# Rotating images by 180 degrees: one group loaded in four interleaved parts, and a store that waits for the third of them

## The chip, the cores and the metric

The kernel runs on one core of a Trainium2 chip. The metric is device time in microseconds (us) of one execution. The profile is one execution of the same program, taken by the hardware profiler; its span is the time from the first to the last instruction, and what lies around the span is in the metric too.

## The reference

```python
def setup_inputs():
    batch, c, h, w = 32, 3, 256, 256
    return {"x": np.random.randn(batch, c, h, w).astype(np.float32)}

def reference(x):
    return np.rot90(x, k=2, axes=(-2, -1)).astype(np.float32)
```

A rotation by 180 degrees turns both axes of each 256x256 image round. Seen as one line of 65,536 numbers, each of the 96 images is reversed. There is no arithmetic: 25.2 MB are read, reversed and written.

## The kernel before

Each image is cut into four rows of E = 16384 numbers (64 KB), which gives 384 rows. They form three groups of 128 rows, and each group fills one tile of 128 partitions by 16384 columns: A, Bt and Ct (lines 38 to 40). The first two groups take the even and the odd rows of the first 256 (`x4[0]`, `x4[1]`), the third takes the last 128 rows in order (`x4[2]`, line 34). A fourth tile T (128 x 2048, J = 2048) is for exchanging.

Loads: A and then Ct are issued from the SP queue (SyncE), Bt from the ACT queue, each as one transfer over all 128 partitions (lines 64 to 67). A memset of a few columns of Bt (line 65) stands ahead of Bt's load, which waits for it. All three loads are in the queues within the first 2 us.

Reversal: each row of a tile is reversed in place by VectorE. `swap(t, lo, w)` (line 56) exchanges w columns from the left with the w columns at the mirrored place on the right, in three copies: right part reversed into T, left part reversed to the right, T to the left. `turn(t, lo, hi)` (line 69) does this in widths of at most 2048 from the outside inward; `turn(t, 0, half)`, with half = 8192, reverses the whole row. So the last columns that are exchanged are the innermost ones, next to column 8192. All copies are on line 47 and are kept in the order of the program.

Stores: what is left is to turn the order of the four rows of an image, and the output's access pattern does that (line 54, `[:, ::-1, lo:hi]`). All stores are issued from the SP queue, behind the loads of A and Ct. SP is in order: a store that waits holds back the stores behind it.

The order of lines 76 to 84, which is also VectorE's order: three quarters of A (widths 1 to 3); the store of A's first LEAD = 256 columns, which needs only the first width; MID = 2432 columns of Bt; the last width of A; the store of the rest of A (16128 columns); the rest of Bt and its store; Ct and its store.

Of the kernel before, what the change touches and what calls it, by code (L numbers as in the profile page):

```python
# [2 lines left out]

os.environ.setdefault("NEURON_RT_ULTRASERVER_MODE", "4")

# [4 lines left out]


@with_exitstack
def kernel(
    ctx: ExitStack,
    tc: tile.TileContext,
    x: bass.AP,
    out: bass.AP,
):
    nc = tc.nc  # L20
    P = 128

    B, C, H, W = x.shape
    L = H * W
    G = 32
    E = L // 4
    J = E // 8

    xr = x.rearrange("b c h w -> (b c) (h w)").rearrange(
        "m (s e) -> (m s) e", s=4)  # L30
    om = out.rearrange("b c h w -> (b c) (h w)").rearrange(
        "m (s e) -> m s e", s=4)
    rows = 2 * P
    x4 = [xr[0:rows:2], xr[1:rows:2], xr[rows:rows + P]]
    o4 = [om[0:2 * G, 1::2], om[0:2 * G, 0::2], om[2 * G:3 * G]]

    pool = ctx.enter_context(tc.tile_pool(name="slots", bufs=1))
    A = pool.tile([P, E], x.dtype, tag="A")
    Bt = pool.tile([P, E], x.dtype, tag="B")
    Ct = pool.tile([P, E], x.dtype, tag="C")  # L40
    T = pool.tile([P, J], x.dtype, tag="T")

    def back(t, lo, hi):
        return t[:, hi - 1:(lo - 1 if lo else None):-1]

    def copy(dst, src):
        tc.keep_in_program_order(nc.vector.tensor_copy(out=dst, in_=src))  # L47

    def load(t, g, lo, hi, queue=nc.sync):
        return queue.dma_start(out=t[:, lo:hi], in_=x4[g][:, lo:hi])  # L50

    def store(t, g, lo, hi):
        return nc.sync.dma_start(
            out=o4[g][:, ::-1, lo:hi], in_=t[:, lo:hi])

    def swap(t, lo, w):
        hi = E - lo - w
        copy(T[:, 0:w], back(t, hi, hi + w))
        copy(t[:, hi:hi + w], back(t, lo, lo + w))
        copy(t[:, lo:lo + w], T[:, 0:w])  # L60

    MID = 2432
    LEAD = 256
    load(A, 0, 0, E)
    nc.vector.memset(Bt[:, 0:256], 0.0)  # L65
    load(Bt, 1, 0, E, nc.scalar)
    load(Ct, 2, 0, E)

    def turn(t, lo, hi):
        while lo < hi:  # L70
            w = min(J, hi - lo)
            swap(t, lo, w)
            lo += w

    half = E // 2
    turn(A, 0, half - J)
    store(A, 0, 0, LEAD)
    turn(Bt, 0, MID)
    turn(A, half - J, half)
    store(A, 0, LEAD, E)  # L80
    turn(Bt, MID, half)
    store(Bt, 1, 0, E)
    turn(Ct, 0, half)
    store(Ct, 2, 0, E)


# [1 line left out]
_INS = ['x']  # L88
_OUTS = [((32, 3, 256, 256), 'float32')]


# [23 lines left out]
```

## Time and profile before

| | us |
|---|---|
| median of 3 runs (121.79 to 121.88) | 121.8 |
| the profiled execution | 121.81 |
| its span | 120.0 |
| VectorE busy | 44.9 |
| VectorE's wait for the load of A | 38.4 |
| issue of the store of A's first 256 columns | 43.30 |
| issue of the store of the rest of A | 59.62 |
| issue of the store of Bt | 70.37 |
| issue of the store of Ct | 85.50 |

The profile was taken on the one core that runs; PEclk and the like play no part, since TensorE has no work. In the views, "SPq" is SyncE's queue, where DMAs are issued; q1 is the DMA queue fed by SP, q10 the one fed by ACT. In a view by windows, the columns are the window, its length, the busy time of VectorE and GpSimd with the number of instructions in it, the granted clock, the DMA share and the rate. A packet of 64 KB, which is one row, is booked in full in the window in which it starts, so the share of a short window can be above 1 or be 0. The time "to landing" of a DMA runs from the start of its issue to the last of its completion signals.

### The profile page before, as it was taken

To read this page: it belongs to the slowest core of one execution; us is meant where nothing else is said; L and a number is where in the kernel's file an instruction comes from. 1 tells how busy PE (TensorE), PEld (TensorE's weight loads), DVE (VectorE), ACT (ScalarE), POOL (GpSimd) and SP (SyncE) were. 2 spreads that over 40 slices of the span, in tenths; PEclk is the share of its full clock that TensorE was granted. 3 is DMA by queue.
4 is the path that set the end of the run, shared out by engine and by line. 5 is a ranking of instruction groups with operands and counts; after the bars stand their busy time and mean duration, and the time that the engine had idled before them with its cause. 6 is when DMAs were issued, how large, how long until landed. Compare 5 with 4: busy or idle time off the path is not lost.

```text
span 120.0 us, 97 instructions
## 1 busy us (share of the span) xinstructions
DVE 44.9 (37%) x40; POOL 0.2 (0%) x4
## 2 busy tenths in 40 slices
DVE  0000000000000899999999999999400000000000
POOL 0000000000000000000000000000000000000000
DMA  9888988898889888998899777988898889888990
GB/s 349 349 349 349 699 349 349 349 677 371 349 349 677 371 349 349 568 481 349 349 388 688 344 344 344 688 349 349 349 699 349 349 349 699 349 349 349 655 393 0
DMA packets 1008, 50.33 MB, mean 419 GB/s; under 512 B 112, under 2 KB 240, under 8 KB 240
## 3 DMA queue, kind: packets, MB, share of 16 engines
q1 hardware_dynamic: 864, 41.94, 81.4%
q10 hardware_dynamic: 144, 8.39, 16.1%
HBM read 25.17 MB, written 25.17 MB: 419 GB/s over the span
## 4 chain that ended last, share of the span: by engine, by line
DVE 38%; DMA 32%; issue 1%
DMA A<-in_x_dram 32%; DVE T L47 13%; DVE Bt L47 9%; DVE A L47 8%; DVE Ct L47 8%
## 5 line engine op out<-in xcount | busy, mean ns | idle before, releaser
L47 DVE COPY T<-A 128x2048 f32<-128x2048 f32 x4 | 4.9, 1227 | 38.5 <-DMA A<-in_x_dram 38.4
L47 DVE COPY Bt<-T 128x2048 f32<-128x2048 f32 (+2 forms) x5 | 5.1, 1014 | 0.2
L47 DVE COPY T<-Bt 128x2048 f32<-128x2048 f32 (+2 forms) x5 | 5.1, 1013 | 0.2
L47 DVE COPY Bt<-Bt 128x2048 f32<-128x2048 f32 (+2 forms) x5 | 5.1, 1013 | 0.2
L47 DVE COPY A<-T 128x2048 f32<-128x2048 f32 x4 | 4.9, 1227 | 0.1
L47 DVE COPY T<-Ct 128x2048 f32<-128x2048 f32 x4 | 4.9, 1227 | 0.1
L47 DVE COPY Ct<-T 128x2048 f32<-128x2048 f32 x4 | 4.9, 1227 | 0.1
L47 DVE COPY A<-A 128x2048 f32<-128x2048 f32 x4 | 4.9, 1227 | 0.1
L47 DVE COPY Ct<-Ct 128x2048 f32<-128x2048 f32 x4 | 4.9, 1226 | 0.1
L65 DVE MEMSET Bt<- 128x256 f32 x1 | 0.3, 272 | 0.8 <-PEq L99 0.8
L99 POOL MEMSET const-bfloat16-1.0<- 128x1 bf16 x1 | 0.1, 101 | 0.0
L99 POOL MEMSET const-uint8-127<- 128x1 uint8 x1 | 0.1, 101 | 0.0
L99 POOL MEMSET const-float32-0.0<- 128x1 f32 x1 | 0.1, 98 | 0.2 <-issue 0.2
L99 POOL MEMSET const-float32-1.0<- 128x1 f32 x1 | 0.1, 98 | 0.0
## 6 DMA issues: line engine op xcount, KB each, us to landing
out_dram<-A SPq DMA_DIRECT2D x1, 8064.0 KB, 21.0
out_dram<-A SPq DMA_DIRECT2D x1, 128.0 KB, 18.3
A<-in_x_dram SPq DMA_DIRECT2D x1, 38.8
Bt<-in_x_dram ACTq DMA_DIRECT2D x1, 43.2
Ct<-in_x_dram SPq DMA_DIRECT2D x1, 60.1
out_dram<-Bt SPq DMA_DIRECT2D x1, 29.6
out_dram<-Ct SPq DMA_DIRECT2D x1, 33.7
```

The costliest lines, as they stand in the source:

```text
L47: tc.keep_in_program_order(nc.vector.tensor_copy(out=dst, in_=src))
L65: nc.vector.memset(Bt[:, 0:256], 0.0)
L99: nc = _bacc.Bacc("TRN2", target_bir_lowering=False, num_devices=1)
```

## The change

The constant MID goes; LATE = 6144 and KEY = 384 come in.

The load of Ct, one transfer of 128 rows, becomes four transfers from the same queue: the odd rows (64), rows 2 of 4, that is 2, 6, 10, ... (32), rows 0 of 8 (16) and rows 4 of 8 (16). A row and its partition have the same number, so the partitions that a transfer writes are spaced in the same way.

A is now turned up to its innermost 384 columns on each side ahead of the first store (three widths of 2048 and one of 1664). Then come 2048 columns of Bt, then the last 384 columns of A by hand: two copies, then a copy of eight numbers from Ct's row 0 into T, at columns that the exchange doesn't use, and then the last copy. VectorE runs its copies in order, so that last copy, and the store of the rest of A behind it, come after the landing of rows 0 of 8. The other 6144 columns of Bt follow as before. The small copy's result is not used.

```diff
-    MID = 2432
+    LATE = 6144
     LEAD = 256
+    KEY = 384
     load(A, 0, 0, E)
     nc.vector.memset(Bt[:, 0:256], 0.0)
     load(Bt, 1, 0, E, nc.scalar)
-    load(Ct, 2, 0, E)
+    for first, step in ((1, 2), (2, 4), (0, 8), (4, 8)):
+        nc.sync.dma_start(out=Ct[first::step, :], in_=x4[2][first::step, :])
...
-    turn(A, 0, half - J)
+    turn(A, 0, half - KEY)
     store(A, 0, 0, LEAD)
-    turn(Bt, 0, MID)
-    turn(A, half - J, half)
+    turn(Bt, 0, half - LATE)
+    copy(T[:, 0:KEY], back(A, half, half + KEY))
+    copy(A[:, half:half + KEY], back(A, half - KEY, half))
+    copy(T[0:1, KEY:KEY + 8], Ct[0:1, 0:8])
+    copy(A[:, half - KEY:half], T[:, 0:KEY])
     store(A, 0, LEAD, E)
-    turn(Bt, MID, half)
+    turn(Bt, half - LATE, half)
     store(Bt, 1, 0, E)
```

## The prediction

> **What bounds the kernel now.** I read the page's DMA rows first, because the engines are mostly idle there.
>
> ```profile
> DVE  0000000000000899999999999999400000000000
> DMA  9888988898889888998899777988898889888990
> DMA packets 1008, 50.33 MB, mean 419 GB/s; under 512 B 112, under 2 KB 240, under 8 KB 240
> q1 hardware_dynamic: 864, 41.94, 81.4%
> q10 hardware_dynamic: 144, 8.39, 16.1%
> ```
>
> The two queues fill 97.5% of the sixteen DMA engines' span; VectorE is busy in the middle only. So the chain of waits, which names VectorE for 38% and ends at the last store's issue, misleads: the time is what the DMA engines need for 384 rows in and 384 rows out, 64 KB each. Windows show what one row costs; a row's whole time is booked to the window in which it starts.
>
> ```profile
> core 0: us, DVE busy (x) POOL busy (x), PEclk, DMA share, GB/s
> 1.70:2.20 0.50, 0.00 (x0) 0.00 (x0) 1.00 6.32 2097
> 55.60:56.10 0.50, 0.47 (x2) 0.00 (x0) 1.00 4.54 1966
> 58.00:58.50 0.50, 0.47 (x2) 0.00 (x0) 1.00 4.90 2097
> 60.40:60.80 0.40, 0.40 (x1) 0.00 (x0) 1.00 0.52 177
> 60.80:61.30 0.50, 0.47 (x2) 0.00 (x0) 1.00 5.13 2185
> 101.00:102.00 1.00, 0.00 (x0) 0.00 (x0) 1.00 2.42 1049
> ```
>
> In 101 to 102, 1049 GB/s for 1 us is sixteen rows, one per engine if the work is even; a share of 2.42 over 1 us says each took 2.42 us. The engines go in waves, one row each: 48 x 2.42 = 116.2 us of the 120.0. The rest is the start (the first wave begins at 1.7 and its rows take 6.32 x 0.5 = 3.16 us, 0.74 more), the spread of the engines (0.5 us per wave) and the end. The third group is the eight waves up to the one that starts in 58.0 to 58.5. Behind it come the small rows of the first store (60.4 to 60.8), then the first wave of the large store of A (60.8 to 61.3): no hole at the change from loading to storing. Last, the lines that decide when that store is there:
>
> ```profile
> Ct<-in_x_dram SPq DMA_DIRECT2D x1, 60.1
> 54.66 0.36 DVE L47 COPY T<-Bt 128x384 f32<-128x384 f32 x1
> 55.84 1.23 DVE L47 COPY T<-A 128x2048 f32<-128x2048 f32 x1
> 59.62 0.55 SPq L53 DMA_DIRECT2D out_dram<-A  x1
> 59.62 1.23 DVE L47 COPY T<-Bt 128x2048 f32<-128x2048 f32 x1
> L65 DVE MEMSET Bt<- 128x256 f32 x1 | 0.3, 272 | 0.8 <-PEq L99 0.8
> ```
>
> The store of A is issued at 59.62 and moves data from 60.83, so an issue is worth about 1.2 us of lead. The third load was issued at 1.17 and landed 60.1 later, at 61.27, some 0.4 us after its last rows ended (58.0 to 58.5, plus 4.90 x 0.5 = 2.45).
>
> **The change part by part.** *VectorE's order.* It starts at 39.52 as now. Three widths of 2048 in A are nine copies at a pitch of 1.26 us (11.35), three copies of 1664 at 1.06 (67.19 to 70.37 now: 3.18), three of 2048 in B (3.79), two of 384 at 0.39 (54.66 to 55.84 is three): 58.63. Then comes the new copy of one row of eight numbers. No such copy is in the trace; it lies between nothing and the 0.36 of a 128x384 copy, and I take 0.10, near the 98 ns of GpSimd's smallest memset. The last 384 columns cost 0.39. Without a wait, A is stored from 59.12 instead of 59.62. Behind it stand B's other 6144 columns (9 x 1.26 = 11.35) and C's 15.1. B's store moves from 70.37 to about 71 and C's from 85.50 to about 86; they are needed when the rows before them are through, at about 79.9 and 99.3 (windows in which the next wave starts). Nine and thirteen microseconds of cover: nothing.
>
> *The wait.* At full rate the third part of C (rows 0 of 8) is the wave that starts at 55.6 to 56.1, ends by 58.5 and lands by 58.9. VectorE stands there from 58.63, so it waits 0.25 us; the store is issued at 59.4 and ready at 60.6, while the engines are on rows 4 of 8 until 60.4 to 60.9 and on the small rows until 60.8 to 61.3. Queued behind the waiting copy are the rest of B and all of C on VectorE, and three stores on SP; all have the cover above. Nothing. If the landing were 0.2 us later, the cover would be gone.
>
> *Four transfers for one.* SP issues three more. One issue takes 0.42 us, so they are out by 3 us, and the first row of C is due at 41. The bytes are the same; a completion packet more per engine and transfer lies below what the windows resolve. If each new transfer paid what the very first wave paid, 0.74, it would be 3 x 0.74 = 2.2; but the change from C to A above, with A's queue not empty, shows no such price. I take 0.
>
> *The rate of a sparse transfer.* This is the term that decides. Every 2.42 in the trace is from a transfer over all 128 partitions. The changed load writes 64, 32, 16 and 16 of them, the last two at every eighth partition. The bound from below is 2.42, no price. What speaks against it: a row takes 2.42 us, 27.1 GB/s, whether it is read from memory or written to it (the windows at 58.0 and 101.0), and whether one queue or two are in use. [...] The least sharing there can be is two rows to an entry: 4.84 for a wave. The other end is all four parts so: eight waves, 8 x 2.42 = 19.4. I take two waves, the 16-row ones, since one row per engine leaves them no way to spread over time: 2 x (4.84 - 2.42) = 4.84 us. It is nearer to the row at 2.42 than to the far end.
>
> [...]
>
> Under this the rows 0 of 8 land at 55.6..56.1 + 4.84 + 0.4 = 61.3, A is issued at 61.8 and ready at 63.0, and the rows 4 of 8 run until 65.3: no hole comes on top.
>
> **Sum** against the profiled execution (121.81, span 120.0; the median is 121.8): 0 + 0 + 0 + 4.84 = **126.65 us**, a span of 124.9.
>
> **The rivals.** *No price (23%).* Sparse transfers run at 2.42 and all else is covered: 121.8 to 121.9. For it: the engine alone explains 27.1 GB/s as well.
>
> *A wait too late (17%).* If engines are bound to partitions, rows 0 of 8 are two rows on each of eight engines, and the third part ends with the whole load. No rate is lost, since each engine still has eight rows, but the wait ends at 61.27. A's store is issued at 61.27 + 0.1 + 0.4 = 61.8 and ready at 63.0 instead of 60.83: a hole of 2.1 us, and up to 0.74 more if an idle engine pays again as at 1.7. 123.9 to 124.7, say 124.2. For it: the change hangs the store on one landing; against it: nothing shows how rows are dealt out. [...] No row here shows which engine takes which row.
>
> *More waves at half rate (16%).* If the 32-row part is dealt so too, four waves: 121.8 + 9.7 = 131.5 (7%); if all eight, 141.2 (9%). [...]
>
> *Each new transfer starts anew (6%).* Up to 2.2 us: 122.1 to 124.0.
>
> *Faster (6%).* The windows at 60.4 and 60.8 leave open whether the store of A, issued at 59.62 with 1.2 us of lead, comes a touch late behind the small rows. An issue at 59.4 starts it 0.25 us sooner, and everything behind it: 121.55. It decides only if rows wait for the issue and not for the engines. Against it: the small rows fill that time.
>
> **How the numbers follow.** 32% for the forecast, and 23, 17, 16, 6 and 6. About 0.2%, 0.24 us, is what a measurement can tell from no change. Faster 0.06, within it 0.23, slower 0.71. The likeliest's own range is 126.2 to 127.2. The range over all reaches from the faster case, 121.5, to the four waves at half rate, 131.8; beyond it lies the case of all eight waves and little else.
>
> **What would show it.** Right: windows in which the rows 0 of 8 and 4 of 8 start have a share of about 4.84 per row, and the first wave of A starts near 65.7. Waves of 2.42 throughout with A at 60.8 mean no price; a slice without DMA at 61 to 63 with A issued near 61.8 means the late wait; half-rate waves from 41 on mean the 141. The forecast falls if every wave of C keeps 2.42. VectorE's part is right if it reaches the small copy near 58.6.

## The result and the profile after

The changed kernel takes 127.16 us (median of 5 runs, 126.77 to 127.33) against 121.82 for the kernel before: ratio 1.0432, 95% interval 1.0414 to 1.0451, slower by 5.3 us. The profiled execution took 126.99 with a span of 125.2, against 121.81 and 120.0. The prediction was 126.65, within 121.5 to 131.8.

The windows of the changed kernel in which the waves of the third group's last rows and of A's store start:

```profile
core 0: us, DVE busy (x) POOL busy (x), PEclk, DMA share, GB/s
53.20:53.80 0.60, 0.60 (x1) 0.00 (x0) 1.00 4.18 1748
55.70:56.30 0.60, 0.60 (x1) 0.00 (x0) 1.00 7.62 1748
60.00:61.10 1.10, 0.00 (x0) 0.00 (x0) 1.00 4.17 894
61.10:64.80 3.70, 2.90 (x5) 0.00 (x0) 1.00 0.00 0
64.80:65.40 0.60, 0.60 (x1) 0.00 (x0) 1.00 0.21 38
65.40:66.30 0.90, 0.87 (x2) 0.00 (x0) 1.00 3.16 1268
```

A rate times a window's length gives the rows in it: 1748 GB/s x 0.6 us is sixteen rows of 64 KB, 894 x 1.1 is fifteen. The share is a mean over the sixteen engines, so where sixteen rows start, the share times the length is the time of one row. So the last wave of rows 2 of 4 takes 4.18 x 0.6 = 2.51 us, the rows 0 of 8 take 7.62 x 0.6 = 4.57, and the rows 4 of 8 take 4.17 x 1.1 x 16/15 = 4.89. The empty window from 61.10 to 64.80 is no hole: nothing starts in it because all engines are in the middle of a slow row. The small rows of the first store follow, and A's first large wave starts at 65.4 instead of 60.8.

The timeline of the same kernel around the waiting copy (start, duration, engine, operation, and the idle time before it with its releaser):

```profile
58.22 0.36 DVE L47 COPY A<-A 128x384 f32<-128x384 f32 x1
61.79 0.16 DVE L47 COPY T<-Ct 1x8 f32<-1x8 f32 x1 [3.21 <-DMA Ct<-in_x_dram]
61.87 0.34 DVE L47 COPY A<-T 128x384 f32<-128x384 f32 x1
62.24 0.58 SPq L53 DMA_DIRECT2D out_dram<-A  x1
73.60 0.54 SPq L53 DMA_DIRECT2D out_dram<-Bt  x1
88.74 0.54 SPq L53 DMA_DIRECT2D out_dram<-Ct  x1
```

VectorE waits 3.21 us, since the rows 0 of 8 are late, but the store it holds back is issued at 62.24, 3.2 us ahead of A's first wave. The three stores are still in time: the first rows of B's, issued at 73.60, start after 84.0, and those of C's, issued at 88.74, after 103.5.

### The profile page after: what moved, and what is told of

Same layout as the page of the kernel before. It is cut to its first block, busy times and chain, and to the rows that moved or that the text cites. A ratio compares the mean times of both kernels' runs of the same rounds, so it can differ in the third digit from the quotient of the medians.

```text
span 125.2 us, 103 instructions
## 1 busy us (share of the span) xinstructions
DVE 45.0 (36%) x41; POOL 0.2 (0%) x4
## 4 chain that ended last, share of the span: by engine, by line
DVE 36%; DMA 31%; another core or an unknown queue 3%; issue 1%
DMA A<-in_x_dram 31%; DVE T L47 12%; DVE A L47 8%; DVE Bt L47 8%; DVE Ct L47 8%
## 5 line engine op out<-in xcount | busy, mean ns | idle before, releaser
L47 DVE COPY T<-A 128x2048 f32<-128x2048 f32 (+2 forms) x5 | 5.1, 1013 | 38.5 <-DMA A<-in_x_dram 38.4
L47 DVE COPY T<-Ct 128x2048 f32<-128x2048 f32 (+1 forms) x5 | 5.1, 1013 | 3.3 <-DMA Ct<-in_x_dram 3.2
L47 DVE COPY A<-A 128x2048 f32<-128x2048 f32 (+2 forms) x5 | 5.1, 1014 | 0.2
L47 DVE COPY A<-T 128x2048 f32<-128x2048 f32 (+2 forms) x5 | 5.0, 1010 | 0.1
L47 DVE COPY Bt<-T 128x2048 f32<-128x2048 f32 x4 | 4.9, 1228 | 0.1
L47 DVE COPY T<-Bt 128x2048 f32<-128x2048 f32 x4 | 4.9, 1227 | 0.1
L47 DVE COPY Bt<-Bt 128x2048 f32<-128x2048 f32 x4 | 4.9, 1226 | 0.1
```

## The experiments

The first question is which part of the change costs: the four transfers, the new order on VectorE, or the wait. Each ratio is to runs of the kernel before that were made together with the run in question; their medians lie between 121.82 and 121.91.

**The split alone**, on the kernel before:

```diff
-    load(Ct, 2, 0, E)
+    for first, step in ((1, 2), (2, 4), (0, 8), (4, 8)):
+        nc.sync.dma_start(out=Ct[first::step, :], in_=x4[2][first::step, :])
```

> The kernel before, with only the load of the third group in four parts; no wait on it, VectorE's order and the store of A as before. If two rows at an entry are the cause (theory): the two 16-row waves take some 4.6 to 4.9 us each instead of 2.42, as in the changed kernel, and the time is 126.8 to 127.3. If the wait is the cause (rival): 121.8 to 122.0, since nothing waits for a part.

126.98 us, ratio 1.0427 (1.0412 to 1.0443), which is the changed kernel's ratio. Windows of this run:

```profile
55.50:56.10 0.60, 0.56 (x2) 0.00 (x0) 1.00 7.77 1748
59.80:61.00 1.20, 1.17 (x2) 0.00 (x0) 1.00 4.10 874
```

The two waves take 7.77 x 0.6 = 4.66 and 4.10 x 1.2 = 4.92 us. The split carries the whole loss, with nothing waiting for it.

**The order alone**, on the changed kernel:

```diff
-    for first, step in ((1, 2), (2, 4), (0, 8), (4, 8)):
-        nc.sync.dma_start(out=Ct[first::step, :], in_=x4[2][first::step, :])
+    load(Ct, 2, 0, E)
...
-    copy(T[0:1, KEY:KEY + 8], Ct[0:1, 0:8])
```

> The changed kernel with the third group in one load and without the small copy, so without the wait; only VectorE's new order is left. Theory: 121.8 within 0.1, the store of A is issued near 59.0 and the rows behind it start when the engines are free, at 60.8 as before. If the order costs something by itself: above 122.1.

121.97 us, ratio 1.0014 (1.0004 to 1.0024); the store of A is issued at 59.19. That lies between the two times expected: the order costs about 0.15 us, by the interval at most 0.3, which I don't explain.

**The wait, on the whole load** (the changed kernel with one load, the small copy kept):

```diff
-    for first, step in ((1, 2), (2, 4), (0, 8), (4, 8)):
-        nc.sync.dma_start(out=Ct[first::step, :], in_=x4[2][first::step, :])
+    load(Ct, 2, 0, E)
```

> The changed kernel with the third group in one load; the small copy is kept and now waits for the whole load. It lands at 61.27, the small copy takes 0.08 at its pitch and the last copy 0.37, so the store of A is issued near 61.75 and moves data 1.2 us later, at 62.95 instead of 60.83. Theory (a late wait has a price of its own, which the changed kernel did not pay): a hole of 2.1, 123.9, up to 124.7 if the idle engines start slowly. Rival (something else covers it): 121.8 to 122.0.

123.84 us, ratio 1.0175 (1.0158 to 1.0192), a loss of 2.0. Windows of this run:

```profile
60.40:61.20 0.80, 0.00 (x0) 0.00 (x0) 1.00 0.48 164
61.20:62.80 1.60, 1.55 (x3) 0.00 (x0) 1.00 0.00 0
62.80:63.10 0.30, 0.27 (x2) 0.00 (x0) 1.00 8.07 3441
```

Only small rows start from 60.4 to 61.2, nothing from 61.2 to 62.8, and A's first wave comes at 62.8 to 63.1. Unlike the empty window of the changed kernel this one is a hole: the last load's rows, which start between 58.0 and 58.4 and take 2.49 us, ended before it. The store was issued at 61.66, and 1.2 us of lead put it where it is. The first wave after the hole takes 8.07 x 0.3 = 2.42, so idle engines did not start slowly here. The late wait of the rivals has the price that was worked out for it; the changed kernel doesn't pay it, because its last wave covers the time.

**A wait on a part, split by columns** (the changed kernel with two loads over all partitions):

```diff
-    for first, step in ((1, 2), (2, 4), (0, 8), (4, 8)):
-        nc.sync.dma_start(out=Ct[first::step, :], in_=x4[2][first::step, :])
+    load(Ct, 2, 0, 14336)
+    load(Ct, 2, 14336, E)
```

> The changed kernel with the third group in two loads over all 128 partitions, columns 0 to 14335 and then 14336 to 16383; the small copy waits for the first. The first part is 8 rows of 56 KB per engine, 8 x 2.12 = 16.9 us from 41.1 to 41.6, so it lands near 58.9 and VectorE, at the small copy from 58.6, hardly waits. Theory (only the spacing of the partitions costs): 121.8 to 122.0, with the same kind of wait as in the changed kernel. If a second transfer or a wait on a part has a price: above 122.2.

121.97 us, ratio 1.0012 (1.0003 to 1.0021). The small copy waits 0.30 us and the store of A is issued at 59.43. The order alone took the same 121.97, so a wait on a part adds nothing that shows if the part lies in the columns and not in the partitions.

The second question is what makes the two 16-row waves slow: their size, or their partitions.

**Odd and even rows**, and **three parts**, both on the kernel before:

```diff
-    load(Ct, 2, 0, E)
+    for first, step in ((1, 2), (0, 2)):
+        nc.sync.dma_start(out=Ct[first::step, :], in_=x4[2][first::step, :])
```

> The kernel before, with the third group loaded as odd rows and then even rows, 64 each. Theory (cost only where the sixteen rows that are on the way at once meet at entries): as in the changed kernel the odd rows go at 2.42 to 2.5 and the even rows do too, 121.8 to 122.1. Rival (a transfer over fewer partitions is slow as such): all eight waves slower, 131 or more.

> The kernel before, with the third group as odd rows, rows 2 of 4 and rows 0 of 4 (64, 32, 32). Theory: the 32-row parts keep 2.42 to 2.5 a wave, as rows 2 of 4 did in the changed kernel, so 121.9 to 122.2. If price grows steadily with the number of parts (rival): about two thirds of the changed kernel's 5.3, near 125.

The second has `((1, 2), (2, 4), (0, 4))` in the loop. 121.84 us, ratio 1.0003 (0.9992 to 1.0014), and 122.02 us, ratio 1.0001 (0.9983 to 1.0020): no loss with 64 rows or with 32.

**Lower and upper half**, the same two transfers of 64 rows with other partitions together:

```diff
-    load(Ct, 2, 0, E)
+    for first in (0, 64):
+        nc.sync.dma_start(out=Ct[first:first + 64, :], in_=x4[2][first:first + 64, :])
```

> The kernel before, with the third group loaded as partitions 0 to 63 and then 64 to 127. The same two transfers of 64 rows as odd and even rows; only which partitions are together differs. Theory: if each half reaches half of the entries, all eight waves take 4.84, 8 x 2.42 = 19.4 more: 141.2. Rival (only number and size of the transfers count): the same time as odd and even rows. [...]

143.0 us, ratio 1.1735 (1.1713 to 1.1757). Windows of the first and the third of the eight waves:

```profile
41.00:41.50 0.50, 0.50 (x1) 0.00 (x0) 1.00 9.30 2097
50.40:51.60 1.20, 1.17 (x2) 0.00 (x0) 1.00 4.27 874
```

The waves take 9.30 x 0.5 = 4.65 and 4.27 x 1.2 = 5.12 us. There are sixteen rows in each window, two transfers of 64 rows and the same bytes as with odd and even rows, and the times are 21.2 us apart. So it is which partitions are on the way together. The 141.2 that was expected is 1.8 too low: it took every wave at 4.84, and waves like the third take 5.12.

**Sets of partitions by themselves.** The transfers of one kernel, one behind the other:

```python
def put(parts, rows):
    nc.sync.dma_start(out=A[parts, :], in_=xr[rows, :])
...
put(slice(0, 128), slice(0, 128))
put(slice(0, 64, 4), slice(0, 16))
put(slice(32, 96, 4), slice(0, 16))
put(slice(64, 128, 4), slice(0, 16))
put(slice(0, 128, 8), slice(0, 16))
put(slice(0, 128, 8), slice(0, 128, 8))
put(slice(0, 16), slice(0, 16))
...
```

> A measurement, not a rotation: no reversal, and most of the output is not written. Transfers one after the other, each waiting for the one before, rows of 64 KB, into one tile: all 128 rows; then sixteen rows to partitions 0 to 60 by 4, to 32 to 92 by 4, to 64 to 124 by 4, to 0 to 120 by 8 (from neighbouring rows, then from rows 8 apart), to 0 to 15; 64 rows to 0 to 63 and to 0 to 126 by 2; 32 rows to 0 to 124 by 4; and two stores of sixteen rows, from 0 to 60 by 4 and from 32 to 92 by 4. If entries go by partition (theory), sets of sixteen rows differ though they move the same rows: some take 2.42, some 4.84, some 9.7, and the rows' spacing in memory is nothing. If size or spacing counts (rivals): all sets of sixteen take the same, or the one from rows 8 apart takes longer than the one from neighbouring rows. [...]

Windows, each round the start of one wave: the last wave of all 128; 0 to 60 by 4; 32 to 92 by 4; 64 to 124 by 4; by 8 from neighbouring rows; by 8 from rows 8 apart; 0 to 15; the second wave of 0 to 63; the third wave of 0 to 126 by 2; the second wave of 0 to 124 by 4; then the stores from 0 to 60 by 4 and from 32 to 92 by 4. VectorE has no column here.

```profile
core 0: us, POOL busy (x), PEclk, DMA share, GB/s
19.20:19.90 0.70, 0.00 (x0) 1.00 3.46 1498
24.00:25.00 1.00, 0.00 (x0) 1.00 4.32 983
31.30:32.30 1.00, 0.00 (x0) 1.00 2.79 1050
36.60:37.50 0.90, 0.00 (x0) 1.00 5.24 1165
44.00:45.00 1.00, 0.00 (x0) 1.00 4.74 1049
51.50:52.00 0.50, 0.00 (x0) 1.00 9.88 2097
58.70:59.80 1.10, 0.00 (x0) 1.00 7.69 953
75.50:76.50 1.00, 0.00 (x0) 1.00 5.12 1049
99.20:100.00 0.80, 0.00 (x0) 1.00 3.02 1311
109.40:110.40 1.00, 0.00 (x0) 1.00 2.42 1049
114.20:114.80 0.60, 0.00 (x0) 1.00 7.95 1748
126.10:126.40 0.30, 0.00 (x0) 1.00 8.19 3495
```

In the same order a row takes 2.42, 4.61, 2.79, 4.72, 4.74, 4.94, 8.46, 5.12, 2.42, 2.42, 4.77 and 2.46 us. The second, third and fourth decide it: the same sixteen rows, the same spacing of 4, only the first partition differs, and 32 to 92 is quick while 0 to 60 and 64 to 124 are slow. Size is out, spacing too. An engine that had to do two of the sixteen rows is out as well: in the window from 36.60 to 37.50 all sixteen start within 0.9 us, so none waits for another to end, and each still takes 4.72. Rows 8 apart in memory add 0.2 at most (4.94 against 4.74). The two stores differ in the same way, 4.77 against 2.46, so it holds in both directions. The 2.79 is a first wave of a load after a pause, as was the 3.16 of the very first wave in the kernel before; the store from 32 to 92, after a pause too, took 2.46.

The sets fall into three groups. All 128, 32 to 92 by 4, 0 to 126 by 2 and 0 to 124 by 4 take 2.4 to 2.8 us a row; 0 to 60 by 4, 64 to 124 by 4, both sets by 8 and 0 to 63 take 4.6 to 5.1; 0 to 15 takes 8.5. Two rows one after the other at 2.42 each would take 4.84 and four 9.7. The lone wave to 0 to 15 took less, 8.46, and the lone waves of the middle group took 4.61 to 4.94; in the second of the four waves of 0 to 63 a row took 5.12. So the middle group is near two rows one after the other; whether rows share something, as the expectation supposed of its entries, and what in a partition's number decides it, no run shows.

The third question came from the kernel before: what would its store of A do without care for its time?

**The plain order**, on the kernel before:

```diff
-    turn(A, 0, half - J)
-    store(A, 0, 0, LEAD)
-    turn(Bt, 0, MID)
-    turn(A, half - J, half)
-    store(A, 0, LEAD, E)
-    turn(Bt, MID, half)
+    turn(A, 0, half)
+    store(A, 0, 0, E)
+    turn(Bt, 0, half)
```

> The kernel before without the small store and without interleaving: all of A is reversed, then stored in one transfer, then B, then C; one load of the third group, no wait. The store of A is issued near 39.52 + 15.1 = 54.6, five microseconds before the engines are free for it. Theory (the engines take their queue in order and full waves are all that counts): the small rows, 0.39 us of the engines for what would be 8 x 0.04 = 0.3 in large rows, are saved, and the time is 121.7 to 121.9, not to be told from before. Rival (a store that is queued early disturbs the loads ahead of it, which the waiting copy was to avoid): above 122.1.

123.0 us, ratio 1.0089 (1.0066 to 1.0111): my theory fell. Windows of this run, the last two waves of loading and the first of storing:

```profile
55.50:58.00 2.50, 2.43 (x3) 0.00 (x0) 1.00 0.97 419
58.00:58.70 0.70, 0.67 (x2) 0.00 (x0) 1.00 4.92 1498
61.30:62.00 0.70, 0.70 (x1) 0.00 (x0) 1.00 3.47 1498
```

The last wave of the load takes 4.92 x 0.7 = 3.44 us instead of 2.45. The wave before it, which also starts after the store's issue at 54.78, takes 0.97 x 2.50 = 2.42, and the store's first wave is normal. No engine is idle (rows that start from 58.0 to 58.7 and take 3.44 end between 61.4 and 62.1, and the store's start from 61.3 to 62.0): the load's last wave itself is slower. Two more kernels separate the missing small store from the early issue: the small store kept with A finished ahead of B, and the kernel before with one store of A at its late time.

```diff
     turn(A, 0, half - J)
     store(A, 0, 0, LEAD)
-    turn(Bt, 0, MID)
     turn(A, half - J, half)
     store(A, 0, LEAD, E)
-    turn(Bt, MID, half)
+    turn(Bt, 0, half)
```

> The kernel before with the small store kept and all of A reversed ahead of B, so that the large store of A is issued near 54.6 instead of 59.62 and lies behind the small one in the queue for five microseconds. If the small rows between the last load and the first large store are what keeps the last load's wave at 2.45 (first reading of the plain kernel, whose last wave took 3.44 with large rows right behind it): 121.8 to 122.0. If an early issue as such slows the last load: about 122.9, with a last wave near 3.4.

```diff
     turn(A, 0, half - J)
-    store(A, 0, 0, LEAD)
     turn(Bt, 0, MID)
     turn(A, half - J, half)
-    store(A, 0, LEAD, E)
+    store(A, 0, 0, E)
```

> The kernel before without the small store: A is stored in one transfer, issued at 59.6 as before. It has no row to move until 60.8, after the loads ended at 60.4 to 60.9. First reading (large rows queued behind the last load cost 1.0): they come too late to disturb, there is a hole of up to 0.4 at first, and the time is 121.7 to 122.1. Rival (the change from loading to storing costs about 1 us wherever no small rows are between): 122.6 to 123.0.

122.85 us, ratio 1.0071 (1.0050 to 1.0091), and 122.17 us, ratio 1.0019 (1.0009 to 1.0030). So it is mostly the early issue: with the small store in place the time is still 1.0 us above before, and a late issue without the small store costs 0.2 to 0.3, a little more than my first reading gave it and well below its rival's 122.6. That first reading, that the small rows shield the load, fell with the first of the two kernels. Windows of that kernel, whose large store is issued at 54.68:

```profile
33.80:34.40 0.60, 0.00 (x0) 0.00 (x0) 1.00 4.18 1748
51.00:51.50 0.50, 0.50 (x1) 0.00 (x0) 1.00 5.27 2097
58.60:59.10 0.50, 0.50 (x1) 0.00 (x0) 1.00 6.17 2097
```

The last wave of loading takes 6.17 x 0.5 = 3.08 us, against 2.45 before and 3.44 in the plain order. This execution took 123.13, the longest of its kernel's four (122.72 to 123.13), and its rows were slower earlier too: 4.18 x 0.6 = 2.51 in the wave at 33.8 and 5.27 x 0.5 = 2.64 in the wave at 51.0, both over before the store's issue. So the last wave holds 0.6 of the 1.3 us that it lost, and at least a part of the rest has another source, which I can't name.

The last wave of loading in the kernel with one store of A at its late time:

```profile
57.90:58.70 0.80, 0.77 (x2) 0.00 (x0) 1.00 3.03 1311
```

It takes 3.03 x 0.8 = 2.42 us: with large rows next in the queue, but issued late, the load keeps its rate. Why the wave ahead of an early store is slower is open.

## Why the prediction was right

**What bounds the kernel.** The sixteen engines' rows, as read: the time moved by what two waves of rows cost and by a wider spread of the engines, while 3.2 us of waiting on VectorE cost nothing: the split alone, without the wait, took as long.

**The rate of a sparse transfer.** The deciding term, taken as two waves at 4.84, is right in kind and place: 4.57 and 4.89 in the changed kernel, 4.66 and 4.92 with the split alone. That the odd rows and the rows 2 of 4 would keep their rate was a choice, and the runs with 64 and 32 rows bear it out. The reason given for it, that several rows per engine can spread over time and one cannot, is not what decides: 0 to 63 has four rows per engine and is slow, and 32 to 92 by 4 has one and is quick. In that respect the choice of just these two waves was partly luck. The 4.84 itself was my estimate, two rows of 2.42 one after the other at what the prediction calls an entry. No run shows such an entry, and the 27.1 GB/s in both directions don't prove one; what the runs show in its place is that the partitions decide: by 4 from 0 and from 64 a row takes 4.61 and 4.72, from 32 it takes 2.79.

**Its size.** 4.84 forecast, 5.18 between the profiled executions. The two waves themselves cost a little less than forecast, 4.57 + 4.89 - 2 x 2.42 = 4.62. The sum left out two things that the windows show: the rows ahead of the two waves ran slightly slower in this execution (2.51 for the last wave of rows 2 of 4, against 2.42), and the engines spread wider, 65.4 to 66.3 at A's first wave against 60.8 to 61.3, so that the last engine is 5.0 us later. With the split alone the slower rows are not seen (3.46 x 0.7 = 2.42 for the same wave, in the window from 53.0 to 53.7); the spread is (A's first wave from 65.3 to 66.3). The two errors have opposite signs, so a part of the total's closeness is luck.

**The wait.** Forecast: landing at 61.3, issue at 61.8, no hole. Measured: the wait ended at 61.79 and the issue came at 62.24. The lag from the last data to the landing was under-sized, since I took 0.4 from the load before, and here rows that start by 56.3 and take 4.57 ended 0.9 ahead of 61.79; nothing hung on it. That a landing 0.2 us later would take away the cover at full rate was not tried as such; the wait on the whole load shows what is lost when the cover is gone, 2.0 against the 2.1 worked out.

**VectorE's order, four transfers for one.** Nothing, as costed: 58.6 was forecast for the small copy's place in line, and the copy ahead of it began at 58.22 and took 0.36. The small copy takes 0.08 of VectorE's time line (61.79 to 61.87), close to the 0.10 taken.

**The rivals.** No price: false. The late wait: false here, since all sixteen rows 0 of 8 start between 55.7 and 56.3, so that none waits for another on its engine; two rows on each of eight engines was a supposition, and no run shows which engine takes which row. Its price is nearly right when the wait is on the whole load. More waves at half rate: false for these sets; true for the lower and upper half, 143.0 us. A new start for each transfer: false, by the odd and even rows, 121.84, and the three parts, 122.02. Faster: false.

**What the prediction lacked.** It treated the moment of A's issue as free on the early side. It isn't: five microseconds earlier went with 1.0 to 1.1 us more on the kernel before, nearly all of it in the last wave of loading in the plain order, and about half of it there in the profiled execution with the small store kept. With the split alone the store also lay in the queue six microseconds ahead of the end of the loads, and no price was seen beside the half-rate waves; whether those hide it is open.

## What to carry to other kernels

When a load that the DMA engines are bound by is cut into parts, cut it along the columns, which took the same 121.97 us here as one load in the same order, or time each part's set of partitions by itself: with sixteen rows, 0 to 60 by 4 took 4.61 us a row and 32 to 92 by 4 took 2.79; with 64 rows, 0 to 63 took 5.12 and 0 to 126 by 2 took 2.42. Count the waves, not the bytes: two of 48 waves at half rate were 4.6 of the 5.2 us. And price a moved issue on both sides: the store that was issued at 61.66 left a hole and 2.0 us more, and with one that was issued five microseconds early the last wave of the load ahead of it was slower, 3.44 and 3.08 us against 2.45.

## What was not expected of the hardware

With A's store queued five microseconds early, the last wave of the load ahead of it took 3.44 us in the plain order and 3.08 with the small store kept, instead of 2.45; with a late issue and no small store it took 2.42. With partitions 0 to 63, where slow waves follow one another, a row takes more than twice the usual time, 5.12 against 2 x 2.42 = 4.84, though in the lone waves of the sets by 4 and by 8 the slow rows took 4.6 to 4.9.
